# Lower halves of 34 expert tiles split beside the mixers and kept in DRAM, with 34 early first products in layer 0 and 16 of their results in DRAM

## The chip, the cores and the metric

The kernel runs on one core of one Trainium2 chip. The metric is the device time in microseconds of one execution. The kernel before takes 3050.3 us (median of 3 runs, 3050.26 to 3050.61).

## What the reference computes

The reference is a two-layer backbone (`DEPTH = 2`) over 256 latent and 256 context tokens of width 1024. Each layer modulates and normalises the tokens, projects them, runs four token mixers side by side, gates and sums their outputs, and then runs PEER, a retrieval over 16384 single-neuron experts in a 128 x 128 grid of product keys. Layer 0 treats all 512 tokens in PEER, layer 1 the 256 latent ones. The part that matters here:

```
s = einsum('thpd,hpnd->thpn', q, keys);  sv, si = top_k(s, 16)       # 8 heads, two lists of 128 keys
best, pos = top_k(sums of the two lists, 16);  g = softmax(best)     # 16 experts of each head
act = gelu(einsum('tkd,td->tk', u_tab[ec], xc))                      # first product, with U
out = einsum('tk,tkd->td', gc * act, v_tab[ec])                      # second product, with V
```

The kernel does not gather the rows of most tokens. It treats the experts as 128 tiles of 128. For each tile it forms the first product of all its tokens with all 128 experts, multiplies the gelu of it by a gate that is zero where an expert was not chosen, and adds the second product. In layer 0, 384 of the 512 tokens go this way; the first 128 tokens go by gathering their rows, on GpSimd and VectorE (`gather`).

## The kernel before

**Numbers.** Every fp32 matrix is split into an upper half `wh` (rounded to fp32r by a ScalarE copy) and a lower half `wl` (the rest, by a VectorE subtraction). A product is three fp32r matmuls: upper by upper, upper by lower, lower by upper (`mm3`, L391 to L393). So every 512 KB weight tile that arrives in the buffer `wraw` costs one ScalarE and one VectorE instruction of 128 x 1024 before TensorE can use it. `wraw`, `wh` and `wl` have three buffers each.

**Stages of a layer.** First the mixers with their projections, then an output projection (`out`), queries (`wq`), routing, and the expert loop. Instructions are issued engine by engine in an order that a scheduler fixes when the program is built; each engine and each DMA queue then runs its own row in that order.

- *Mixers (layer 0: up to about 570 us).* A list made by `unit_order` names the weight tiles in the order of use: `na`, `gqa`, `dif`, then 32 `gate` tiles with `hyn` among them, and from gate 0 on one `modr` tile (a row block of the modulation matrix, consumed by VectorE at L513) behind each gate. `Units.load` (L305) brings them into `wraw` on the SP queue; `Units.split` (L328, L329) makes the halves, for some tiles on GpSimd, which takes longer.
- *Routing (layer 0: about 643 to 873 us).* Per group of 128 tokens VectorE ranks keys (`lists`, `top16`), picks experts (`select`), and builds one-hot matrices (`hot`, L1501, `gated`, L1517) from which TensorE scatters the gates (`scatter`, L1539), which ScalarE evacuates into `gblk` and SP stores to `gd`. Beside it `early` runs first products as a filler: one call of `u_next` per step of the routing. `u_next` loads a tile of U (L1227), splits it (L1230, L1231), multiplies 24 matmuls of 384 columns and takes the gelu (L1257) into one of `ne` result buffers. `NE = (20, 50)` limits the early products of layer 0 to 20: 10 buffers of their own and 10 in `hT`, which is free at that time.
- *Expert loop (layer 0: from about 873 us).* For j in 0..127: load V and the gates, multiply gelu by gate (L1666), split the result and V, 18 matmuls of 512 columns for the second product (L1677), and `u_next` for a tile further on, when a result buffer is free and the tile is at most `own + ...` ahead. Behind the split of V a few steps of `gather` are taken: two per j, and every second j a third from j = 25 on. A step of `gather` issues a row gather on GpSimd's queue and adds or dots an earlier one on VectorE (L1307, L1311); three buffers `grow`.

Of the kernel before, what the change touches and what calls it, by code (L numbers as in the profile page):

```python
# [8 lines left out]
F32 = mybir.dt.float32  # L9
# [10 lines left out]
P = 128  # L20
# [44 lines left out]

def unit_order():

    o = []
    for l in range(DEPTH):
        o += [(l, 'na', i) for i in range(6)]  # L70
        o += [(l, 'gqa', i) for i in range(4)]
        o += [(l, 'dif', i) for i in range(6)]
# [69 lines left out]
def lay_out(i):  # L142
# [59 lines left out]
    a['W'] = np.stack([U[k] for k in dict.fromkeys(order)])  # L202
# [57 lines left out]
NE_BUF = (10, 18)  # L260
NE_OWN = (10, 34)
NE = (20, 50)
# [4 lines left out]
def body(ctx, tc, I, out, dbg=None):  # L267
# [26 lines left out]
    place = {k: z for z, k in enumerate(dict.fromkeys(order))}  # L294

    class Units:
# [4 lines left out]
        def load(self, upto):  # L301
            while self.loaded < min(upto, len(order)):
                m = self.loaded
                self.raw[m] = wp.tile([P, D], F32, name="wraw", bufs=3)
                sp.dma_start(self.raw[m], I['W'][place[order[m]]])  # L305
# [12 lines left out]
        def split(self, upto):  # L318
            while self.split_to < min(upto, len(order)):
# [9 lines left out]
                (pool if order[m][1] == 'wq' or order[m][:2] == (1, 'na') and order[m][2] < 2 or order[m][0] == 0 and order[m][1] in ('gate', 'hyn') and order[m][2] % 2 and (order[m][1] == 'hyn' or order[m][2] < 20) else dve).tensor_tensor(lo, r, h.bitcast(F32), op=ALU.subtract)  # L329
                self.hl[m] = (h, lo)  # L330
# [7 lines left out]
        def next(self, kind):  # L338
            assert order[self.n][1] == kind, (order[self.n], kind)

            end = kind == 'wq' and order[self.n + 1:self.n + 2] != [(order[self.n][0], kind, (order[self.n][2] + 1) % 8)]
            self.split(self.n + (1 if end else 2))
# [229 lines left out]
    for l in range(DEPTH):  # L572
# [647 lines left out]
        assert own == nbuf or last  # L1220
        gd = [dr.tile([NB, P, 32, 32], F32, name=f"gd{l}_{z}") for z in range(4)]
        us, ur, gas = {}, {}, {}
# [10 lines left out]
        def split_u(j):  # L1233
# [3 lines left out]
            lo = wp.tile([P, D], F32R, name="wl", bufs=3)  # L1237
            halves(h, lo, ur.pop(j), lo_eng[0])
            us[j] = (h, lo)

        def u_mm(j):
# [97 lines left out]
        with ExitStack() as tx:  # L1339
# [238 lines left out]
            def routing():  # L1578
# [46 lines left out]
        with ExitStack() as dx:  # L1625
# [29 lines left out]

            def gate(j):
# [3 lines left out]
                if z < own:  # L1660
# [45 lines left out]
            mrows = mod_rows()  # L1706
            load_v(0)
# [4 lines left out]
            for j in range(P):  # L1712
                load_v(j + 2)
                load_g(j + 4)

# [115 lines left out]
```

## Time and profile before

| What | Value |
|---|---|
| median of 3 runs | 3050.3 us |
| the profiled execution | 3045.44 us, its span 3043.6 us |
| TensorE (PE) busy | 2934.7 us, 96% |
| VectorE (DVE) busy | 2270.8 us, 75% |
| ScalarE (ACT) busy | 1457.9 us, 48% |
| GpSimd (POOL) busy | 515.4 us, 17% |
| DMA | 661.95 MB, mean 217 GB/s |
| granted TensorE clock, mean | 0.988 |

The share of busy time is a mean over stages with different limits. Matmuls overlap in the pipeline, so the time that one costs TensorE is the distance from its start to the start of the next, which is shorter than its duration; a stretch in which PE is shown busy all the time can therefore still have room.

### The profile page before, as it was taken

Reading aid. Unit: us, or ns where it says so; the run is one execution under the profiler, and the core shown is the slowest. Engines: PE = TensorE matmul, PEld = TensorE weight load, DVE = VectorE, ACT = ScalarE, POOL = GpSimd, SP = SyncE. Lnnn points to the kernel's source line nnn. Section 1 sums busy time; section 2 is a strip of 40 time slices with the busy share of each in tenths; the row PEclk is TensorE's granted clock in tenths of the full one; section 3 lists DMA queues with packets and bytes.
Section 4 is the critical chain, followed back from the end, with each engine's and each line's share of the span. In section 5 each row is a group of like instructions: output and inputs, shape, how many; then the busy total and the mean of one; then the engine's idle time right before and its main releaser. Section 6 shows DMA issues by size and latency. Waiting matters only on the chain.

```text
span 3043.6 us, 47372 instructions
## 1 busy us (share of the span) xinstructions
PE 2934.7 (96%) x17500; PEld 2595.1 (85%) x17500; DVE 2270.8 (75%) x4818; ACT 1457.9 (48%) x2583; POOL 515.4 (17%) x374
## 2 busy tenths in 40 slices
PE   8999999988899999999999998999899999999998
PEld 6877777888799999999999986888898989989986
DVE  5775877799988777778777686789699667555545
ACT  5444422558853333333333334465548754555443
POOL 1001100220023444434444101000160000000000
PEclk9999999999999999999999998999999999999999
DMA  7232345534489998898998864357655699766644
GB/s 273 74 103 85 111 140 163 177 99 173 160 309 341 332 322 302 309 333 313 316 321 311 280 190 140 91 181 223 198 164 199 214 298 307 227 208 208 210 149 146
DMA packets 263032, 661.95 MB, mean 217 GB/s; under 512 B 21480, under 2 KB 114160, under 8 KB 262288
## 3 DMA queue, kind: packets, MB, share of 16 engines
q1 hardware_dynamic: 222336, 513.88, 51.4%
q0 software_dynamic: 40464, 145.05, 13.8%
q8 instruction: 137, 2.24, 0.3%
q14 instruction: 95, 0.78, 0.1%
HBM read 609.56 MB, written 49.29 MB: 216 GB/s over the span
## 4 chain that ended last, share of the span: by engine, by line
PE 68%; DVE 11%; DMA 4%; issue 2%; ACT 2%; POOL 0%; DVEq 0%; ACTq 0%; SPq 0%; POOLq 0%
PE mm L1677 13%; PE at L1677 13%; PE po L393 9%; PE po L391 9%; PE po L392 9%; PE mm L391 4%; PE mm L392 4%; PE mm L393 4%; PE at L1539 3%; DMA vr<-in_V_dram 2%; DMA wraw<-in_W_dram 2%; DVE wl L1231 1%; DVE wl L329 1%; ACT vh L1230 1%; DVE rep L1364 1%
## 5 line engine op out<-in xcount | busy, mean ns | idle before, releaser
L393 PE MATMUL po<-nh,wl 128*128 128x384 f32 (+1 forms) x2048 | 635.7, 311 | 10.6 <-DVE wl L1231 10.5
L391 PE MATMUL po<-nh,wh 128*128 128x384 f32 (+1 forms) x2048 | 638.0, 312 | 7.3 <-ACT wh L1230 3.5
L1230 ACT ACTIVATE wh<-wraw 128x1024 fp32r<-128x1024 f32 x256 | 270.5, 1058 | 338.8 <-PE po L392 283.7
L1230 ACT ACTIVATE vh<-vr 128x1024 fp32r<-128x1024 f32 x254 | 269.7, 1062 | 304.5 <-DMA vr<-in_V_dram 265.6
L391 PEld LDWEIGHTS po<-nh,wh 128*128 128x128 f32 x2048 | 390.5, 191 | 17.0 <-ACT wh L1230 4.5
L393 PEld LDWEIGHTS po<-nh,wl 128*128 128x128 f32 x2048 | 390.1, 191 | 13.8 <-DVE wl L1231 13.1
L1231 DVE TENSOR_TENSOR vl<-vr,vh 128x1024 fp32r<-128x1024 f32 x254 | 310.2, 1221 | 110.3 <-ACT vh L1230 110.1
L1231 DVE TENSOR_TENSOR wl<-wraw,wh 128x1024 fp32r<-128x1024 f32 x241 | 293.6, 1220 | 114.3 <-ACT wh L1230 113.9
L391 PE MATMUL mm<-nh,wh 128*128 128x256 f32 (+1 forms) x1056 | 346.7, 330 | 12.2 <-ACT nh L488 3.9
L392 PE MATMUL po<-nl,wh 128*128 128x384 f32 x1024 | 344.6, 337 | 0.0
L393 PE MATMUL mm<-nh,wl 128*128 128x256 f32 (+1 forms) x1056 | 341.8, 325 | 0.4 <-POOL wl L329 0.4
L392 PE MATMUL mm<-nl,wh 128*128 128x256 f32 (+1 forms) x992 | 324.3, 328 | 0.2 <-DVE nl L472 0.2
L328 ACT ACTIVATE wh<-wraw 128x1024 fp32r<-128x1024 f32 x156 | 164.7, 1058 | 291.1 <-PE mm L392 166.4
L392 PE MATMUL po<-nh,wh 128*128 128x256 f32 x1024 | 289.8, 283 | 0.0
L1300 POOL DMA_INDIRECT grow<-in_UR_dram,gix x128 | 173.8, 1358 | 481.2 <-DVE gix L1473 240.4
L1677 PE MATMUL mm<-vl,Wh 128*128 128x512 f32 x635 | 250.2, 394 | 4.3 <-DVE vl L1231 4.2
L1677 PE MATMUL mm<-vh,Wh 128*128 128x512 f32 x635 | 248.3, 391 | 1.6 <-ACT vh L1230 1.6
L1677 PE MATMUL at<-vh,Wl 128*128 128x512 f32 x635 | 248.5, 391 | 0.0
L1677 PE MATMUL at<-vh,Wh 128*128 128x512 f32 x635 | 248.2, 391 | 0.0
L1677 PE MATMUL mm<-vh,Wl 128*128 128x512 f32 x635 | 247.5, 390 | 0.0
L1677 PE MATMUL at<-vl,Wh 128*128 128x512 f32 x635 | 247.1, 389 | 0.0
L391 PEld LDWEIGHTS mm<-nh,wh 128*128 128x128 f32 x1056 | 203.5, 193 | 38.5 <-ACT nh L471 4.7
(367 smaller groups left out, 6200.7 us busy)
## 6 DMA issues: line engine op xcount, KB each, us to landing
wraw<-in_U_dram SPq DMA_DIRECT2D x256, 512.0 KB, 4.5
vr<-in_V_dram SPq DMA_DIRECT2D x254, 512.0 KB, 4.6
wraw<-in_W_dram SPq DMA_DIRECT2D x214, 512.0 KB, 3.8
gd<-gblk SPq DMA_DIRECT2D x80, 512.0 KB, 4.5
G<-gd SPq DMA_DIRECT2D x32, 768.0 KB, 8.1
G<-gd SPq DMA_DIRECT2D x32, 512.0 KB, 5.4
grow<-in_W_dram SPq DMA_DIRECT2D x24, 512.0 KB, 4.5
mw<-in_W_dram SPq DMA_DIRECT2D x16, 512.0 KB, 9.3
```

The costliest lines, as they stand in the source:

```text
L328: act.activation(h, r, AF.Copy)
L329: (pool if order[m][1] == 'wq' or order[m][:2] == (1, 'na') and order[m][2] < 2 or order[m][0] == 0 and order[m][1] in ('gate', 'hyn') and ...
L391: pe.matmul(ps, w[0], x[0], start=first, stop=False)
L392: pe.matmul(ps, w[0], x[1], start=False, stop=False)
L393: pe.matmul(ps, w[1], x[0], start=False, stop=last)
L1230: act.activation(h, r, AF.Copy)
L1231: return eng.tensor_tensor(lo, r, h.bitcast(F32), op=ALU.subtract)
L1300: pool.indirect_dma_start(out=q[-1], out_offset=None, in_=tab, in_offset=bass.IndirectOffsetOnAxis(ap=gix[:, p, e:e + 1], axis=0))
L1364: dve.match_replace(rep[:, :nn], v[:, 0:8], x, -3e38)
L1539: pe.matmul(ps4[:, :, z], A[:, :, z], C[:, z, :, h], start=h == 1, stop=h == 0)
L1677: pe.matmul(accs[i][h], w[a][:, i * 128:(i + 1) * 128], v[b][:, h * 512:(h + 1) * 512], start=j == 0 and a + b == 0, stop=j == P - 1 and a ...
```

## The change

- `unit_order` puts 34 units `('pre', j)` between the projection tiles of layer 0: one before each of `na` 1 to 5, `gqa` 0 to 3, `dif` 0 to 5, `hyn` 0 to 5, and `gate` 12 to 24. A `pre` unit loads tile j of U, splits it like any other (ScalarE copy, VectorE subtraction), and stores the lower half to DRAM (`ulo_d`). Its upper half is dropped.
- In routing, `load_u` brings, for j below 34, the tile of U on SP's queue and the stored lower half on GpSimd's queue into `wl`; `split_u` then makes only the upper half, on ScalarE.
- The early first products of layer 0 go from 20 to 34: `NE` is now 18 (8 own buffers and 10 in `hT`), and the gelu of the first 16 goes through a tile `gs` (two buffers) to DRAM (`ga_d`). The expert loop loads them back, two iterations ahead (`load_ga`).
- The steps of `gather` are spread anew: one per j for j from 2 to 19, then 2 or 3 (two of three j's take 3).

```diff
+N_PRE = (34, 0)
         for i in range(32):
             if i == 8:
-                o += [(l, 'hyn', i) for i in range(6)]
-            o += [(l, 'gate', i)]
+                o += proj('hyn', 6)
+            o += [(l, 'pre', j) for j in [next(pre, None) if 11 < i < 28 else None] if j is not None] + [(l, 'gate', i)]
...
-NE_BUF = (10, 18)
-NE_OWN = (10, 34)
-NE = (20, 50)
+NE_BUF = (8, 18)
+NE_OWN = (8, 34)
+NE = (18, 50)
+
+NE_OUT = (16, 0)
...
+                if order[m][1] == 'pre':
+                    sp.dma_start(ulo_d[order[m][0]][order[m][2]], lo.bitcast(F32))
+                    continue
...
         def load_u(j):
                 sp.dma_start(ur[j], I['U'][l, j])
+                if j < N_PRE[l]:
+                    ul[j] = wp.tile([P, D], F32R, name="wl", bufs=3)
+                    pool.dma_start(ul[j], ulo_d[l][j])
...
+            if j < N_PRE[l]:
+                lo = ul.pop(j)
+                act.activation(h, ur.pop(j), AF.Copy)
+            else:
...
+            if j < nout:
+                ga = up.tile([P, nd], F32, name="gs", bufs=2)
+                tables.append(act.activation(ga, ps[:, :nd], AF.Gelu))
+                sp.dma_start(ga_d[j], ga)
+                return
...
-                    fill.add(early(own + 2048 // nd))
+                    fill.add(early(nout + own + 2048 // nd))
...
-                        fill.add(early(ne - 2 if NG else ne))
+                        fill.add(early(nout + ne - 2 if NG else ne))
-                fill.add(early(ne))
+                fill.add(early(nout + ne))
...
+            def load_ga(j):
+                if j < nout:
+                    gas[j] = None, up.tile([P, nd], F32, name="gs", bufs=2)
+                    sp.dma_start(gas[j][1], ga_d[j])
...
-                        for _ in range((2 if j > 1 else 0) + (j > 24 and j % 2)):
+                        for _ in range((j > 1) if j < 20 else 2 + (j % 3 > 0)):
```

Three places in the order of the built programs follow. The line numbers of the changed kernel are some 30 higher.

ScalarE in the last scatter of layer 0, in the kernel before (`gblk` is the evacuation of scattered gates, `wh` the upper half of a U tile, `hT<-po` the gelu of a first product into `hT`):

```order
L1541 ACTIVATE gblk<-at 128x128x4 x2
L1515 ACTIVATE ohC<-ohB,gT 128x128
L1545 ACTIVATE gacc<-gblk 128x64
L1515 ACTIVATE ohC<-ohB,gT 128x128 x3
L1541 ACTIVATE gblk<-at 128x128x4 x8
L1545 ACTIVATE gacc<-gblk 128x64
L1230 ACTIVATE wh<-wraw 128x1024
L1257 ACTIVATE hT<-po_8994 128x384
```

The same place in the changed kernel:

```order
L1571 ACTIVATE gblk<-at 128x128x4 x2
L1260 ACTIVATE wh<-wraw 128x1024
L1287 ACTIVATE hT<-po_9354 128x384
L1571 ACTIVATE gblk<-at 128x128x4 x2
L1260 ACTIVATE wh<-wraw 128x1024
L1287 ACTIVATE hT<-po_9414 128x384
L1545 ACTIVATE ohC<-ohB,gT 128x128 x4
```

Where eight evacuations stood in a row with no product between them, every two are now followed by a product. On TensorE the first second product stands behind 527 matmuls of first products (22 tiles) before, and behind 816 (34 tiles) now.

SP's queue beside the gates 12 to 24, before (`wraw<-in_W` brings a gate or modulation tile, `wbraw` a branch tile):

```order
L305 DMA wraw<-in_W_dram 128x1024 x2
L308 DMA wbraw<-in_WB_dram 128x256
L305 DMA wraw<-in_W_dram 128x1024 x3
L308 DMA wbraw<-in_WB_dram 128x256
L305 DMA wraw<-in_W_dram 128x1024 x2
```

And now (`ulo` is the stored lower half of a U tile):

```order
L341 DMA ulo_26_95<-wl 128x1024
L315 DMA wraw<-in_U_dram 128x1024
L315 DMA wraw<-in_W_dram 128x1024 x2
L318 DMA wbraw<-in_WB_dram 128x256
L341 DMA ulo_27_96<-wl 128x1024
L315 DMA wraw<-in_U_dram 128x1024
```

Each gate now has three tiles through the three `wraw` buffers where it had two, and a store that waits for a VectorE subtraction stands ahead of the loads.

VectorE a few iterations into the expert loop, before (`vl` is the lower half of V, `Wl` that of the gated gelu, `grow,gdot` a gathered row):

```order
L1307 SCALAR_TENSOR_TENSOR grow,gdot<-grow,mtok 128x1024 x2
L1231 TENSOR_TENSOR wl<-wraw,wh 128x1024
L1666 TENSOR_TENSOR ga<-ga,G_9149 128x384
L1231 TENSOR_TENSOR vl<-vr,vh 128x1024
L1231 TENSOR_TENSOR Wl<-ga,Wh 128x384
```

And now:

```order
L1337 SCALAR_TENSOR_TENSOR grow,gdot<-grow,mtok 128x1024
L1703 TENSOR_TENSOR gs<-gs,G_9921 128x384
L1252 TENSOR_TENSOR vl<-vr,vh 128x1024
L1252 TENSOR_TENSOR Wl<-gs,Wh 128x384
```

For its first 21 iterations the loop now holds second products alone on TensorE (378 matmuls in a row), one gathered row in each, and no split of U.

## Rows read from the trace of the kernel before

**Rows 1.** The page: busy us, share of the span and instructions of the engines.
```profile
PE 2934.7 (96%) x17500; PEld 2595.1 (85%) x17500; DVE 2270.8 (75%) x4818; ACT 1457.9 (48%) x2583; POOL 515.4 (17%) x374
```

**Rows 2.** Busy time by stretch of layer 0 (columns: first row).
```profile
core 0: us, PE busy (x) PEld busy (x) DVE busy (x) ACT busy (x) POOL busy (x), PEclk, DMA share, GB/s
36.00:170.00 134.00, 130.24 (x852) 105.69 (x850) 96.44 (x313) 69.55 (x151) 11.60 (x19) 1.00 0.36 106
336.00:450.00 114.00, 109.80 (x503) 87.06 (x502) 92.75 (x194) 38.69 (x66) 11.73 (x5) 0.97 0.41 129
643.00:668.00 25.00, 17.83 (x104) 16.59 (x103) 25.00 (x122) 10.54 (x16) 0.00 (x0) 0.88 0.20 64
668.00:723.00 55.00, 45.35 (x334) 41.52 (x334) 51.10 (x179) 50.12 (x141) 0.00 (x0) 0.96 0.40 144
723.00:780.00 57.00, 53.66 (x365) 49.90 (x362) 51.63 (x192) 45.96 (x120) 0.00 (x0) 0.97 0.46 167
780.00:805.00 25.00, 21.95 (x149) 19.87 (x148) 21.02 (x87) 19.39 (x48) 0.00 (x0) 0.93 0.41 148
805.00:873.00 68.00, 61.79 (x426) 58.88 (x423) 65.36 (x211) 48.25 (x108) 0.00 (x0) 0.95 0.57 217
873.00:1798.00 925.00, 924.94 (x4677) 840.53 (x4676) 712.97 (x917) 333.29 (x455) 346.38 (x256) 1.00 0.89 311
1798.00:1823.00 25.00, 25.00 (x113) 20.79 (x112) 23.93 (x46) 10.08 (x15) 0.00 (x0) 1.00 0.60 188
```

**Rows 3.** Timeline of TensorE in the expert loop: second product, first product, second product.
```profile
1500.50 0.39 PE L1677 MATMUL mm<-vh,Wh 128*128 128x512 f32 x1
...
1504.59 0.34 PE L391 MATMUL po<-nh,wh 128*128 128x384 f32 x1
...
1508.75 0.39 PE L1677 MATMUL mm<-vh,Wh 128*128 128x512 f32 x1
```

**Rows 4.** Timeline of TensorE: first first product, first second product of layer 0.
```profile
642.85 0.34 PE L391 MATMUL po<-nh,wh 128*128 128x384 f32 x1
...
873.35 0.50 PE L1677 MATMUL mm<-grow,Wh 128*128 128x512 f32 x1
```

**Rows 5.** Groups of instructions, 640 to 870 us: busy us, mean ns, idle before.
```profile
L1539 PEld LDWEIGHTS <-ohA 128*128 128x128 f16 x768 | 85.6, 139 | 26.2 <-issue 18.1 <-DVE ohA L1501 6.3 <-DVE ohC L1517 0.5
L1231 DVE TENSOR_TENSOR wl<-wraw,wh 128x1024 fp32r<-128x1024 f32 x22 | 26.6, 1212 | 1.1 <-ACT wh L1230 1.1
```

**Rows 6.** The splits of weights beside the mixers, 36 to 450 us.
```profile
L329 DVE TENSOR_TENSOR wl<-wraw,wh 128x1024 fp32r<-128x1024 f32 x32 | 39.0, 1220 | 20.8 <-ACT wh L328 20.7
L328 ACT ACTIVATE wh<-wraw 128x1024 fp32r<-128x1024 f32 x45 | 47.6, 1058 | 99.0 <-issue 45.6 <-PE mm L392 40.5 <-PE mm L393 8.2
```

**Rows 7.** Upper halves and VectorE's longest wait, 336 to 450 us.
```profile
L328 ACT ACTIVATE wh<-wraw x12: 1051/1060/1064, 336.2 to 443.6; 128x1024 fp32r<-128x1024 f32 x12
DVE junk L513 <- DMA wraw<-in_W_dram: 10.2, 5, 3.5
```

**Rows 8.** DMA of 336 to 450, of 880 to 950, of 1800 to 1824 us.
```profile
wraw<-in_W_dram SPq DMA_DIRECT2D x25, 512.0 KB, 3.8
...
DMA packets 13465, 24.08 MB, mean 344 GB/s; under 512 B 697, under 2 KB 8583, under 8 KB 13461
vr<-in_V_dram SPq DMA_DIRECT2D x10, 512.0 KB, 6.9
grow<-in_UR_dram,gix POOLq DMA_INDIRECT x21, 7.3
...
vr<-in_V_dram SPq DMA_DIRECT2D x3, 512.0 KB, 4.0
```

**Rows 9.** VectorE in the expert loop, 870 to 1800 us.
```profile
L1307 DVE SCALAR_TENSOR_TENSOR grow<-grow,mtok 128x1024 f32<-128x1024 f32 x128 | 154.4, 1221 | 82.8 <-DMA grow<-in_UR_dram,gix 82.8
L1231 DVE TENSOR_TENSOR Wl<-ga,Wh 128x384 fp32r<-128x384 f32 x102 | 56.3, 552 | 13.0 <-ACT Wh L1230 12.8
```

**Rows 10.** DMA on GpSimd's queue beside the mixers, 36 to 170 us.
```profile
qk<-in_cst_dram POOLq DMA_DIRECT2D x1, 512.0 KB, 11.3
```

More of the change, by code (lines that the diff above doesn't have):

```diff
@@ L69, in unit_order @@
     for l in range(DEPTH):
-        o += [(l, 'na', i) for i in range(6)]
-        o += [(l, 'gqa', i) for i in range(4)]
-        o += [(l, 'dif', i) for i in range(6)]
+        pre = iter(range(N_PRE[l]))
+        proj = lambda kind, n: [x for i in range(n) for x in [(l, 'pre', j) for j in ([] if kind == 'na' and i == 0 else
+                                                                                       [next(pre, None)]) if j is not None] + [(l, kind, i)]]
+        o += proj('na', 6)
+        o += proj('gqa', 4)
+        o += proj('dif', 6)
         for i in range(32):
             if i == 8:
-                o += [(l, 'hyn', i) for i in range(6)]
-            o += [(l, 'gate', i)]
+                o += proj('hyn', 6)
+            o += [(l, 'pre', j) for j in [next(pre, None) if 11 < i < 28 else None] if j is not None] + [(l, 'gate', i)]
             if N_MOD1 + i < (N_MOD2 if l else N_MOD):
@@ L201, in lay_out @@
     order = unit_order()
-    a['W'] = np.stack([U[k] for k in dict.fromkeys(order)])
+    a['W'] = np.stack([U[k] for k in dict.fromkeys(order) if k[1] != 'pre'])
     a['WB'] = np.stack(WB)
@@ L293, in body @@
     order = unit_order()
-    place = {k: z for z, k in enumerate(dict.fromkeys(order))}
+    place = {k: z for z, k in enumerate(k for k in dict.fromkeys(order) if k[1] != 'pre')}
+    ulo_d = [[dr.tile([P, D], F32, name=f"ulo{l}_{j}") for j in range(N_PRE[l])] for l in range(DEPTH)]
     class Units:
@@ L304, in load @@
                 self.raw[m] = wp.tile([P, D], F32, name="wraw", bufs=3)
-                sp.dma_start(self.raw[m], I['W'][place[order[m]]])
+                sp.dma_start(self.raw[m], I['U'][order[m][0], order[m][2]] if order[m][1] == 'pre' else I['W'][place[order[m]]])
                 if order[m][1] == 'gate':
@@ L338, in next @@
         def next(self, kind):
+            if order[self.n][1] == 'pre':
+                self.split(self.n + 2)
+                self.n += 1
             assert order[self.n][1] == kind, (order[self.n], kind)
             end = kind == 'wq' and order[self.n + 1:self.n + 2] != [(order[self.n][0], kind, (order[self.n][2] + 1) % 8)]
-            self.split(self.n + (1 if end else 2))
+            self.split(self.n + (1 if end else 2 + (order[min(self.n + 1, len(order) - 1)][1] == 'pre')))
             if not end:
@@ L1220, in body @@
         assert own == nbuf or last
+        nout = NE_OUT[l]
         gd = [dr.tile([NB, P, 32, 32], F32, name=f"gd{l}_{z}") for z in range(4)]
-        us, ur, gas = {}, {}, {}
+        us, ur, ul, gas = {}, {}, {}, {}
+        ga_d = [dr.tile([P, nd], F32, name=f"ga{l}_{z}") for z in range(nout)]
         def load_u(j):
@@ L1236, in split_u @@
             h = wp.tile([P, D], F32R, name="wh", bufs=3)
-            lo = wp.tile([P, D], F32R, name="wl", bufs=3)
-            halves(h, lo, ur.pop(j), lo_eng[0])
+            if j < N_PRE[l]:
+                lo = ul.pop(j)
+                act.activation(h, ur.pop(j), AF.Copy)
+            else:
+                lo = wp.tile([P, D], F32R, name="wl", bufs=3)
+                halves(h, lo, ur.pop(j), lo_eng[0])
             us[j] = (h, lo)
@@ L1659, in gate @@
                 z, ga = gas.pop(j)
-                if z < own:
+                if z is None:
+                    pass
+                elif z < own:
                     free.insert(0, z)
@@ L1706, in body @@
             mrows = mod_rows()
+            load_ga(0)
+            load_ga(1)
             load_v(0)
@@ L1714, in body @@
                 load_g(j + 4)
+                load_ga(j + 2)
                 while nu[0] < min(P, j + own + (ne - own) * max(0, 64 - j) // 64) and free:
```

## Prediction

> **What bounds the kernel now.** The page comes first: TensorE is busy 96% of the span [rows 1], so only a stage in which it has room can pay for anything. The busy time by stretch, read second, finds that room [rows 2]. In the expert loop PE is shown busy 924.94 of 925 us. In routing (643 to 873 us) it is VectorE that is full: 25.00 of 25, 51.10 of 55, 51.63 of 57, 21.02 of 25, 65.36 of 68 us, 214.1 of 230 together.
>
> How much room TensorE really has there takes the pitch of its matmuls, from the timeline, third. A second product of one tile runs from 1500.50 to 1504.59, a first product from there to 1508.75: 4.09 and 4.16 us [rows 3]. The 768 scatter matmuls keep the weight loader busy 85.6 us [rows 5]. Routing lasts from the first first product at 642.85 to the first second product at 873.35, 230.5 us [rows 4]; in it stand 22 first products (91.5 us), the scatter (85.6) and some 5 us of small matmuls: 182 us. So 48 us of TensorE lie open in routing, on a stage that VectorE sets. 26.6 us of VectorE's time there are 22 subtractions of U's lower half [rows 5].
>
> **The change part by part.**
>
> *First products moved into routing.* 34 tiles instead of 22 are done before the first second product, 12 more, so the expert loop after it holds 12 x 4.16 = 49.9 us less of TensorE. As TensorE has no gap in that loop [rows 2], this comes off in full: -49.9.
>
> *Routing grows by less than that.* I go by stretches. Up to 805 us the four stretches take 162 us with 148.8 us of VectorE, 92% [rows 2]. 16 of the 22 subtractions lie there (about 18.3 us of the 26.6); without them VectorE has 130.5 us, at the same 92% 142 us. TensorE's own work there is 15 first products (62) and 512 scatter matmuls (57) and a little more, 122 us, and fits. The last scatter now has 19 first products beside 256 scatter matmuls: 19 x 4.16 + 256 x 85.6/768 = 79.0 + 28.5 = 107.5 us, and 2 for its ends, where TensorE sets the pace instead of VectorE (the ranking of the last group of tokens moves up into it). Sum 142 + 110 = 252 us against 230.5: +22. From below, TensorE's work alone is 34 x 4.16 + 85.6 + 5 = 232 us, +2; VectorE at its old share with nothing saved by overlap gives 260, +30. I take +22, since the middle stretches stay VectorE's.
>
> *The stores and loads of 16 gelus* (192 KB each) lie beside TensorE's 4 to 6 us per product in routing; the covers are two `gs` buffers and DMA shares of 0.41 to 0.57 there [rows 2]. Zero; if that cover is gone it is the case of the late halves below.
>
> *The loop's first 21 iterations* are second products alone, 4.09 us each. VectorE needs 1.22 (lower half of V) + 2 x 0.55 + 1.3 (a gathered row) = 3.6 us of that [rows 6, 9], still below. The loads are nearer: V 512 KB, the returned gelu 192, a quarter of the gates' 768, a gathered row 512, together 1.44 MB in 4.09 us, 353 GB/s; from 880 to 950 us the DMA engines moved 344 GB/s on the mean [rows 8]. And V has two buffers: landing (6.9 us under that load, 4.0 in the quiet tail [rows 8]), the copy 1.06, the subtraction 1.22 and the issue make 6.6 to 9.5 us for two iterations, 3.3 to 4.8 each. Bounds: 0, and 21 x 0.7 = 15. At the end of the loop TensorE runs second products alone with no gap, 113 matmuls in 25.00 us [rows 2], but at 188 GB/s. I take 0.3 an iteration, +6, between the two landings.
>
> The Trainium skill ("DMA: Bandwidth & Descriptors", section "Where 436 GB/s comes from") puts the HBM's limit for one core near 358 GB/s, which binds between HBM and SBUF. By that figure 353 GB/s would just pass and this term would be 0 from bandwidth; by the row's 344 GB/s bandwidth alone costs 2 us. The trace's mean agrees with the figure as a ceiling.
>
> *The rest of the loop.* Rows are gathered at 2.67 per iteration instead of 2.5; VectorE already waits 0.65 us for each (82.8 over 128) [rows 9]. Its work per iteration of 8.25 us rises by 0.17 x 1.3 = 0.2 us. Hidden as long as the split of V runs one iteration ahead, as now. Zero, at most 95 x 0.14 = 13.
>
> *34 tiles of U beside the mixers.* Each costs 1.22 us of VectorE and 1.06 of ScalarE [rows 6], a 512 KB load and store on SP. VectorE has cover of 38 us in 36 to 170 us (15 tiles, 18 us) [rows 2]; the six at `hyn` lie in 240 to 290 us, after which the gates follow. The dear place is gates 12 to 24. There VectorE is busy 92.75 of 114 us [rows 2] and a gate comes every (443.6 - 336.2)/11 = 9.8 us [rows 7]; 13 tiles add 15.9 us, so VectorE goes from 81% to 95%. Two buffer rings get tighter as well. Behind a gate's load stood one other tile in the three `wraw`; now all three are taken in each period, so the load of a gate waits for the split of the one before it: landing 3.8 [rows 8], copy 1.06, subtraction 1.22, issue 0.4, about 6.5 us plus VectorE's lag, against 9.8. And ScalarE's copy of the next `pre` tile waits for TensorE to leave the gate before (now it waits like that for one two gates back). Queued behind on SP is the store that waits for a subtraction, with the loads of the next three tiles after it; TensorE waits for those. VectorE loses 10.2 us here to such landings already, in five waits [rows 7]. I take 0.6 us for each of the 13 gates, 8, and 4 for the start, where weights and 5 tiles of U share the queue: +12. Below: 0, all covered. Above: all VectorE time on the path, 34 x 1.22 = 41.5, and 4: 45.
>
> Sum: -49.9 + 22 + 6 + 0 + 12 = -9.9 us. The profiled execution took 3045.44 us (span 3043.6 and 1.8 around it), so it would take 3035.5; the median of the runs stands 4.9 above it at 3050.3, so the forecast is **3040.4 us**.
>
> **The rivals.**
>
> *The mixers cover all* (chance 0.22). VectorE's shares of 72% and 81% speak for it, the waits on landings in [rows 7] against it. With 0 there, 1 in the loop and routing at +20: -29, 3021 us.
>
> *Gates 12 to 24 become bound by VectorE and the `wraw` ring* (0.17). One mechanism: VectorE, filled to 95%, lags; every lag delays the split, that the next load, that the next split. It decides when the lag passes 9.8 - 6.5 = 3.3 us, or when VectorE's lost landings double. Price at the upper bound, 45: -49.9 + 22 + 6 + 45 = +23, 3073 us, slower than before. The saturated stretch speaks for it; that TensorE already idles little there speaks against.
>
> *The loop starves* (0.10). V alone goes at 4.8 us per iteration and the denser gathers lag: 15 + 13 beside 12 and 22: +12, 3062 us. For it: 344 GB/s with landings of 6.9 us. Against it: no gap of TensorE in that load today.
>
> *The lower halves come late, so that the early products are not early* (0.06). They come on GpSimd's queue; `wl` has three buffers, so the load of tile j+2 starts when product j-1 ends, and between back-to-back products (4.16 us each, some 9 in a row in the middle of routing) it has 8.3 us. A 512 KB load on that queue took 11.3 us once [rows 10], row gathers 7.3 [rows 8]. At 11.3 nine products wait 3 us each: +27, 3067 us. The skill gives such a rule ("SBUF — State Buffer", in "The DVE blocks DMA trap (SWDGE)"): descriptors of GpSimd's queue aren't written while VectorE holds the port pair they share. No row here shows it.
>
> *Savings and costs cancel* within 6 us, with none of these: 0.05.
>
> **How the numbers follow.** The forecast has 0.40; its own range is 3028 to 3053. A change below 0.2% (6 us) can't be told from none. Faster by more: 0.22 + 0.40 x 0.75 + 0.02 = 0.54. Within: 0.40 x 0.2 + 0.05 + a share of the starved loop and late halves, 0.19. Slower: the rest, 0.27. The range of 8 in 10 leaves out the upper half of the saturated gates and the lower part of full cover: 3017 to 3067 us.
>
> **What would show it.** Routing, from the first first product to the first second product, takes 252 us, with VectorE near 75% in it. The first 21 second products come every 4.4 us. `na` to `wq` end 12 us later, and the gap is at gates 12 to 24, in VectorE's waits for `wraw`. The forecast is wrong if the first first product starts over 25 us later than 642.85, or if routing takes over 265 us.

## The result and the profile after

The changed kernel takes 3079.61 us (median of 5 runs, 3070.81 to 3087.26), the kernel before 3050.26 (5 runs, 3045.99 to 3050.61). The ratio is 1.0098, 95% interval 1.0080 to 1.0117: slower by 29 us, where 3040.4 was forecast and the range ended at 3067. The profiled execution has a span of 3077.8 us against 3043.6, so 34.2 us more.

First the page: the engines, and the chain that ended last (by engine, then by line).

```profile
PE 2954.4 (96%) x17500; PEld 2605.3 (85%) x17500; DVE 2279.5 (74%) x4818; ACT 1487.0 (48%) x2617; POOL 536.8 (17%) x408
...
PE 59%; DVE 11%; issue 11%; DMA 5%; POOL 5%; ACT 3%; SPq 0%; POOLq 0%; DVEq 0%; ACTq 0%
PE mm L1714 9%; PE at L1714 9%; PE po L409 7%; PE po L407 7%; PE po L408 7%; POOL grow L1330 4%; PE mm L407 4%; PE mm L408 4%; PE mm L409 4%; PE at L1569 3%; DMA wraw<-in_W_dram 2%; DMA vr<-in_V_dram 2%; PE at L403 1%; DVE wl L339 1%; DVE rep L1394 1%
```

TensorE's share is the 96% of [rows 1]. What is to be seen is one entry of the chain: `POOL grow L1330`, GpSimd's issue of row gathers, with 4% of the span, and "issue" with 11%. GpSimd is busy 17% of the time, as before, and nothing in a list of busy shares would point to it. In the chain of the kernel before, POOL has 0% and "issue" 2%:

```profile
PE 68%; DVE 11%; DMA 4%; issue 2%; ACT 2%; POOL 0%; DVEq 0%; ACTq 0%; SPq 0%; POOLq 0%
```

Next the turning points, on TensorE's timeline (start us, us, what, idle before): the first product of the `dif` scores, the first first product, the first second product, and one stall inside the loop.

```profile
175.25 0.48 PE L723 MATMUL at<-qk 64*128 64x256 f32 x1
...
666.62 0.34 PE L407 MATMUL po<-nh,wh 128*128 128x384 f32 x1
...
922.37 0.39 PE L1714 MATMUL mm<-grow,Wh 128*128 128x512 f32 x1
...
1288.21 0.39 PE L1714 MATMUL at<-vh,Wl 128*128 128x512 f32 x1
1293.54 0.69 PE L407 MATMUL po<-nh,wh 128*128 128x384 f32 x1 [4.94 <-ACT ga L1287]
1294.02 0.53 PE L408 MATMUL po<-nl,wh 128*128 128x384 f32 x1
...
1297.49 0.34 PE L407 MATMUL po<-nh,wh 128*128 128x384 f32 x1
```

Against [rows 4] the first first product comes 23.8 us later (666.62 for 642.85), the first second product 49.0 later: the mixers lost 23.8, routing 25.3 (255.75 for 230.50). From the first to the last second product layer 0 takes 949.4 us against 967.3, so the loop gives back 17.9. Between the layers 3.2 are added, and layer 1 is as before: 23.8 + 25.3 - 17.9 + 3.2 = 34.4.

The last rows show what a stall costs: TensorE stood 4.94 us, then ran its matmuls in 0.53 us instead of 0.34 until 1297.49. The granted clock of those 4 us is 0.51 (a row of the next fence), the lower of the two levels, 1.2 GHz. That iteration took 15.22 us instead of 8.25, 7.0 for a gap of 5.

Busy time by stretch (columns as in [rows 2]):

```profile
36.00:170.00 134.00, 122.50 (x754) 99.51 (x752) 99.53 (x297) 77.02 (x145) 11.56 (x19) 0.95 0.62 205
667.00:922.00 255.00, 240.26 (x1654) 227.08 (x1654) 198.50 (x775) 192.50 (x455) 17.97 (x33) 1.00 0.72 256
922.00:1010.00 88.00, 82.16 (x350) 65.26 (x349) 67.56 (x105) 31.86 (x42) 19.06 (x19) 0.98 0.99 348
1100.00:1350.00 250.00, 236.44 (x1161) 211.26 (x1159) 188.22 (x277) 77.00 (x109) 112.24 (x82) 0.98 0.91 317
1293.50:1297.50 4.00, 3.96 (x13) 3.96 (x14) 3.38 (x7) 3.21 (x6) 2.23 (x2) 0.51 0.87 305
1400.00:1700.00 300.00, 300.00 (x1528) 274.11 (x1527) 236.90 (x243) 102.30 (x144) 138.94 (x97) 1.00 0.91 318
```

The first row is the mixers' start: PE 122.50 of 134 us for 130.24 in [rows 2], clock 0.95, DMA share 0.62 for 0.36. In routing (second row) TensorE and VectorE changed places: 240.26 and 198.50 of 255 us, and the clock is full. In the loop 1100 to 1350 us has lost its full TensorE, and 1400 to 1700 us, with the same gathers per iteration and the same GB/s, has not.

To place the loss I take each iteration of the loop and subtract 4.08 us for its second product and 4.17 for a first product if it has one. Without stalls the loop is 964.3 us before and 914.2 after, 50.1 less. Left over:

| stalls in layer 0's loop, us | iterations 0 to 19 | 20 to 69 | 70 to the end | all |
|---|---|---|---|---|
| before | 0.5 | 0 | 2.5 | 3.0 |
| after | 9.4 | 25.0 | 0.9 | 35.3 |

The groups of the gathers in 1100 to 1350 us (busy us, mean ns, idle before and its releasers), first on VectorE, then on GpSimd:

```profile
L1337 DVE SCALAR_TENSOR_TENSOR grow<-grow,mtok 128x1024 f32<-128x1024 f32 x82 | 99.5, 1224 | 61.8 <-DMA grow<-in_UR_dram,gix 61.3
...
L1330 POOL DMA_INDIRECT grow<-in_UR_dram,gix x80 | 109.6, 1370 | 135.9 <-DVE grow L1337 129.9 <-issue 6.1
L1330 POOL DMA_INDIRECT grow<-in_V_dram,gix x2 | 2.6, 1309 | 3.4 <-DVE grow L1337 3.4
```

They wait for each other: VectorE for the gathered row, GpSimd for VectorE to free a row buffer. 82 issues in 250 us are 3.05 us a gather. VectorE's 188.22 us of work and its 61.8 of waiting fill the stretch, so the halves of V and U behind a late row come late. The waits of TensorE in the same stretch (us, times, longest):

```profile
PE po L407 <- ACT ga L1287: 6.5, 2, 4.9
PE mm L1714 <- DVE vl L1252: 4.1, 2, 2.8
PE po L409 <- DVE wl L1252: 2.1, 1, 2.1
```

The top line would send a reader to ScalarE's gelu, or to a shortage of result buffers. ScalarE's timeline at the stall shows that the gelu itself stood behind the copy of a V tile whose load came late:

```profile
1291.11 1.06 ACT L1251 ACTIVATE vh<-vr 128x1024 fp32r<-128x1024 f32 x1 [15.01 <-DMA vr<-in_V_dram]
1292.07 1.04 ACT L1251 ACTIVATE wh<-wraw 128x1024 fp32r<-128x1024 f32 x1
1293.02 0.47 ACT L1287 ACTIVATE ga<-po 128x384 f32<-128x384 f32 x1
```

That load was issued at 1276.49 us, right behind a load of 2 MB (`hT`) in SyncE's queue:

```profile
1272.89 3.50 SPq L1765 DMA_DIRECT2D hT<-h  x1
1276.49 0.38 SPq L1668 DMA_DIRECT2D vr<-in_V_dram  x1
```

The stall of iteration 61, 6.7 us, has another last link. The gelu of the gathered products stands in ScalarE's row ahead of the next split of U, and waits there until VectorE has used the last of the 128 gathered rows of U:

```profile
1351.10 0.31 ACT L1344 ACTIVATE gdot<-gdot 128x128 f32<-128x128 f32 x1 [9.02 <-DVE grow L1337]
```

These two stalls hold 13.6 of the 25.0 us. The kernel before has both waits too: there the V load behind `hT` took 13.9 us to land, and that gelu waited 8.75 us, and TensorE lost nothing by either. So a lead that covered them is gone. Whether the late rows took it can't be read from the list of waits; the experiments tell.

### The profile page after: what moved, and what is told of

Read it like the earlier page. It is cut to its first block, busy times and chain, and to the rows that moved or that the text cites. A ratio compares the mean times of both kernels' runs of the same rounds, so it can differ in the third digit from the quotient of the medians.

```text
span 3077.8 us, 47737 instructions
## 1 busy us (share of the span) xinstructions
PE 2954.4 (96%) x17500; PEld 2605.3 (85%) x17500; DVE 2279.5 (74%) x4818; ACT 1487.0 (48%) x2617; POOL 536.8 (17%) x408
## 4 chain that ended last, share of the span: by engine, by line
PE 59%; DVE 11%; issue 11%; DMA 5%; POOL 5%; ACT 3%; SPq 0%; POOLq 0%; DVEq 0%; ACTq 0%
PE mm L1714 9%; PE at L1714 9%; PE po L409 7%; PE po L407 7%; PE po L408 7%; POOL grow L1330 4%; PE mm L407 4%; PE mm L408 4%; PE mm L409 4%; PE at L1569 3%; DMA wraw<-in_W_dram 2%; DMA vr<-in_V_dram 2%; PE at L403 1%; DVE wl L339 1%; DVE rep L1394 1%
## 5 line engine op out<-in xcount | busy, mean ns | idle before, releaser
L1252 DVE TENSOR_TENSOR wl<-wraw,wh 128x1024 fp32r<-128x1024 f32 x207 | 252.5, 1221 | 114.2 <-ACT wh L1251 114.0
L339 DVE TENSOR_TENSOR wl<-wraw,wh 128x1024 fp32r<-128x1024 f32 x151 | 184.0, 1220 | 62.5 <-ACT wh L338 51.3
```

The lines of the kernel that those rows point to most:

```text
L1252: return eng.tensor_tensor(lo, r, h.bitcast(F32), op=ALU.subtract)
```

## The experiments

"Loop" is from the first to the last second product of layer 0, "start" the first first product, both from the profiled execution. Ratios are to the kernel before, on the same chip, with 95% intervals. Medians are of 4 to 12 runs (e16: 2) on several chips, on which the kernel before took 3046.3 to 3051.0 us, so rows are compared by their ratios.

| kernel | median us | ratio | start | loop | stalls 0 to 19 | 20 to 69 | 70 on |
|---|---|---|---|---|---|---|---|
| before | 3050.3 | 1 | 642.8 | 967.3 | 0.5 | 0 | 2.5 |
| changed | 3079.6 | 1.0098 (1.0080 to 1.0117) | 666.6 | 949.4 | 9.4 | 25.0 | 0.9 |
| e1 gathers by pace | 3063.0 | 1.0063 (1.0045 to 1.0080) | 669.9 | 927.4 | 8.9 | 0 | 4.3 |
| e2 old gather rule | 3080.8 | 1.0111 (1.0094 to 1.0128) | 668.2 | 951.9 | 25.1 | 11.7 | 0.9 |
| e3 before, new gather rule | 3068.2 | 1.0076 (1.0060 to 1.0093) | 644.2 | 984.6 | 0.5 | 17.6 | 2.3 |
| e4 nothing beside na, gqa | 3058.1 | 1.0038 (1.0018 to 1.0058) | 651.2 | 949.5 | 9.3 | 22.4 | 3.7 |
| e5 4 row buffers | 3056.8 | 1.0033 (1.0023 to 1.0042) | 665.9 | 927.2 | 8.8 | 3.1 | 0.9 |
| e6 3 V buffers | 3098.4 | 1.0164 (1.0149 to 1.0178) | 669.6 | 983.3 | 8.2 | 39.2 | 21.9 |
| e7 e1 and e4 | 3043.5 | 0.9988 (0.9979 to 0.9997) | 645.5 | 930.8 | 12.3 | 0 | 4.3 |
| e8 e7, middle to DRAM | 3059.5 | 1.0036 (1.0024 to 1.0048) | 646.8 | 953.3 | 12.9 | 10.8 | 15.6 |
| e9 e4, e5, pace of 3 | 3046.6 | 0.9991 (0.9980 to 1.0001) | 648.2 | 933.9 | 10.5 | 0 | 9.3 |
| e10 e5, no gathers to 19 | 3061.5 | 1.0037 (1.0025 to 1.0048) | 670.0 | 931.9 | 4.2 | 0 | 13.4 |
| e11 stores by GpSimd | 3113.8 | 1.0206 (1.0187 to 1.0226) | 700.6 | 951.0 | 11.3 | 24.6 | 1.0 |
| e12 no lower halves | 3079.5 | 1.0093 (1.0075 to 1.0112) | 642.2 | 958.5 | 10.6 | 26.9 | 6.9 |
| e13 9 not stored | 3093.7 | 1.0160 (1.0138 to 1.0183) | 673.2 | 943.6 | 8.0 | 20.4 | 0.9 |
| e14 9 only loaded | 3096.0 | 1.0151 (1.0132 to 1.0169) | 663.4 | 962.4 | 14.8 | 29.0 | 4.4 |
| e15 e4, e5, pace of 2.67 | 3045.0 | 0.9986 (0.9975 to 0.9997) | 649.1 | 926.6 | 8.4 | 2.6 | 1.5 |
| e16 9 loaded by 1/16 | 3086.4 | 1.0116 (1.0072 to 1.0159) | 664.8 | 950.5 | 14.9 | 15.6 | 5.9 |

**The rate of the gathers (e1, e2, e3).**

```
 e1   n0 = nu[0]            # before the loop's first products of this iteration
      pace = (2.67 if nu[0] > n0 else 1) * (j > 1);  credit[0] += pace
-     for _ in range((j > 1) if j < 20 else 2 + (j % 3 > 0)):
+     for _ in range(int(credit[0]) - int(credit[0] - pace)):
 e2 +     for _ in range((2 if j > 1 else 0) + (j > 24 and j % 2)):
 e3 the kernel before with
    +     for _ in range((j > 1) if j < 20 else 2 + (j % 3 > 0)):
```

> The changed kernel, but an iteration of layer 0's expert loop that has no first product asks for 1 row gather instead of 2 or 3. Theory R (gathers are asked for faster than their three row buffers pass them): in the changed kernel's iterations 20 to 63, 117 gathers are asked for in 334 us of matmuls, 2.85 us each, while GpSimd issued one per 3.05 us there (82 in 1100 to 1350 us); 117 x 3.05 - 334 = 23 us of stalls, 26 measured. With 106 gathers, 3.15 us each, under 6 us of them should be left: 3057 us (3052 to 3062). Rival S (result buffers: 8 instead of 10 of the loop's own, and the waits for a gelu in front of first products): gathers play no part, 3079 us, stalls where they were.

> The changed kernel with the old rule of gathers (2 per iteration from the second on, 2 or 3 from the 25th). Theory R: iterations 2 to 23 ask for 46 gathers in 106 us of matmuls and need 46 x 3.05 = 140 us, so some 34 us of stalls come in the first 25 iterations, and those of iterations 30 to 63 go (97 gathers in 297 us, 3.05 us each): 3080 to 3090 us. Rival S: stalls stay at iterations 30 to 63, and the time stays at 3079 us.

> The kernel before with the new rule of gathers alone (1 per iteration to the 19th, then 2 or 3, mean 2.67). Theory R: iterations 20 to 63 ask for 117 gathers in 334 us as in the changed kernel, so up to 23 us of stalls come into a loop that had none: 3065 to 3073 us. Rival S: the kernel before has its 10 result buffers, no stalls, 3050 us.

e1 takes the 25 us of stalls in iterations 20 to 69 away and leaves none there. The stretch of about iterations 20 to 63, 1013 to 1368 us, in e1:

```profile
1013.00:1368.00 355.00, 355.00 (x1787) 321.70 (x1787) 272.78 (x400) 129.81 (x176) 158.94 (x113) 1.00 0.91 320
```

PE is busy 355.00 of 355 us; the changed kernel has 338.63 in the same stretch, at nearly as many gathers (113 and 116). The median of 3063.0 is 6 above the 3057 expected; 3 of them lie in the mixers, which ended later in its profile than in the changed kernel's. By the ratios e1 gains 0.35%, 11 us, where its profiled loop is 22 shorter; single profiles don't resolve that difference. e3 does the reverse: the new rule alone, in the kernel before with its ten result buffers, makes 17.6 us of stalls in the same iterations. e2 moves stalls to the front as theory R has it, though 25 us rather than 34 there, and 12 that were not expected stay behind. Rival S, the result buffers, is out by e1 and e3: they were not touched in either. The chain of the page agrees: POOL has 5% in e3 as in the changed kernel, and 1% in e1.

**Ring or bandwidth (e5, e6).**

```
 both  NE_BUF 8 -> 5, NE_OWN 8 -> 5, NE 18 -> 15, NE_OUT 16 -> 19   (layer 0)
 e5    name="grow", bufs=3  ->  bufs=4 - l
 e6    name="vr", bufs=2 -> bufs=3;  load_v(j + 2) -> load_v(j + 3)
```

> The changed kernel with 4 row buffers for the gathers instead of 3; the room comes from 3 result buffers (5 instead of 8), and 19 results instead of 16 go to DRAM, so 34 first products stay early. Theory R1 (the ring of row buffers: issue 1.4 us, flight about 7 us, VectorE 1.3 us, 9.2 us over 3 buffers = 3.05 us a gather): 4 buffers pass one per 2.3 to 2.5 us, and the 25 us of stalls in iterations 20 to 63 go: 3050 to 3058 us. Rival R2 (the bandwidth of the DMA engines, 0.91 busy there, sets 3.05 us): another buffer only waits longer, the stalls stay within 5 us, 3075 to 3083 us. Rival S (result buffers): with 5 of them more stalls, over 3085 us.

> The changed kernel with 3 buffers for V tiles instead of 2 and the load three iterations ahead, room and DRAM results as in the kernel with 4 row buffers. It is about the 9 us lost in the first 20 iterations, where second products stand alone at 4.08 us. Theory V1 (ring of V buffers: flight about 7 us, ScalarE 1.06, VectorE 1.22, 9.2 us over 2 buffers = 4.6 us an iteration): 3 buffers give 3.1 us and the 9 us go to under 2. Rival V2 (bandwidth: 1.44 MB asked for per 4.08 us, 353 GB/s, at a DMA share of 0.97 to 1.0): they stay at 7 to 10. Iterations 20 to 63 keep 20 to 30 us of stalls by either.

One more row buffer, with fewer result buffers, empties iterations 30 to 69 of stalls without a change of rule. e6 shares its result buffers and keeps 39.2 us of stalls there, so it is the row buffer that does it. GpSimd's gathers and the busy times of e5 in the window shown above:

```profile
L1330 POOL DMA_INDIRECT grow<-in_UR_dram,gix x74 | 109.1, 1475 | 94.2 <-DVE grow L1337 85.0 <-issue 7.6 <-DVE Wl L1252 1.5
L1330 POOL DMA_INDIRECT grow<-in_V_dram,gix x17 | 23.9, 1405 | 25.5 <-DVE gacc L1341 15.2 <-DVE grow L1337 7.9 <-issue 2.4
```

```profile
1100.00:1350.00 250.00, 250.00 (x1261) 226.81 (x1261) 207.29 (x292) 89.70 (x122) 131.90 (x91) 1.00 0.97 354
```

91 gathers instead of 82, one per 2.75 us, at 354 GB/s instead of 317 and with TensorE full. So 317 GB/s at a share of 0.91 was no ceiling: the ring of three buffers was, and R2 falls. The Trainium skill ("DMA: Bandwidth & Descriptors", "Where 436 GB/s comes from") puts one core's HBM limit near 358 GB/s. This row's mean stays under it, but shorter stretches don't: the changed kernel moved 367 GB/s from 922 to 955 us (a row below) and the kernel before 401 from 880 to 897.5. Here, where one core runs, the measurement decides: the figure is no ceiling.

e6 went the wrong way. In the first 20 iterations 8.2 us stay, the number of V2, so a third V buffer isn't what they lacked; but 61 us of stalls come later, on to iteration 110. That one load further ahead of V holds up the rows or U's tiles behind it is a guess; no run separates it.

**The first 20 iterations (e8, e10).**

```
 e8  -     if j < nout:             (in u_mm and load_ga)
     +     if own <= j < own + nout:          ga_d[j] -> ga_d[j - own]
     the limit of first products:  j + own + (nout + ne - own) * max(0, 64 - j) // 64
 e10 (on e5)  pace = (3 if nu[0] > n0 else 1) * (j >= 20)
```

> As the kernel with both mendings, but products 8 to 23 go to DRAM instead of 0 to 15, so that the loop's own 8 buffers come free from iteration 0 and 8 of the first 24 iterations have a first product: fewer second products alone in a row. If the 9 us of the first 20 iterations come from DMA demand of second products alone, they fall to under 5, and the ratio is 0.997 to 0.999 of the kernel before; if from the reload of results from DRAM, they stay and the ratio is as with the two mendings.

> As the kernel with 4 row buffers, but no gathers at all in the first 20 iterations, then 3 (1 in an iteration without a first product). Read are the first 20 iterations only, since the gathers then end late and cost something at the loop's end. Theory T (traffic: V, gates, results from DRAM and a gather are 1.44 MB per 4.08 us, 353 GB/s): without gathers it is 225 GB/s, and of the 9 us lost in iterations 0 to 19 under 2 are left. Rival U (the reload of results from DRAM with two buffers, behind other loads on SyncE's queue): 7 to 9 us stay.

e10 fits neither expectation: 4.2 us are left of e5's 8.8, in this stretch (926 to 1008 us):

```profile
926.00:1008.00 82.00, 79.41 (x345) 63.98 (x344) 50.49 (x72) 30.38 (x41) 2.67 (x2) 1.00 0.87 278
```

The gathers are half of the loss; with them the changed kernel's stretch runs at 348 GB/s and a share of 0.99 (922 to 1010 us above). The other half comes at 278 GB/s, where VectorE waits 9.3 us in all for gates from DRAM and 1.7 for results between 972 and 1004 us. Bandwidth alone doesn't explain either half. The changed kernel's first eight iterations moved 367 GB/s, more than the 353 that theory T counts, with TensorE full; its loss comes behind them, at 336:

```profile
922.00:955.00 33.00, 33.00 (x148) 27.25 (x147) 23.65 (x34) 13.52 (x17) 7.53 (x7) 1.00 1.02 367
955.00:1010.00 55.00, 49.16 (x204) 38.01 (x203) 43.91 (x72) 18.34 (x25) 11.53 (x12) 0.97 0.97 336
```

e8 failed: first products spread over the first 24 iterations brought more stalls, not fewer. Its limit lets the lead fall over 64 iterations, so it has short iterations and full gathers mixed further on; that part stays open.

**The mixers (e4, e11, e12, e13, e14, e16).**

```
 e4  no 'pre' beside 'na' and 'gqa';  beside gates 3 to 10 and 12 to 25
 e11 -     sp.dma_start(ulo_d[...], lo)      +  pool.dma_start(ulo_d[...], lo)
 e12 N_PRE = (0, 0)
 e13 tiles 0 to 8: split, not stored;  halves again in routing
 e14 tiles 0 to 8: loaded, not split;  e16: of each only columns 0 to 63 loaded
```

> The changed kernel, but the 9 lower halves made beside the na and gqa units are made beside gates instead (gates 3 to 10 and 12 to 27; none beside na and gqa). Theory P (the place costs: na and gqa stand where the DMA share rose from 0.48 to 0.75, and lost 16 of the 24 us): the first first product comes at 650 to 658 us instead of 666.6, and the time is 3063 to 3071 us. Rival Q (each tile costs the same wherever it is made): 666 us and 3079 us.

> The changed kernel, but the lower halves made beside the mixers are stored from GpSimd's queue instead of SyncE's. Theory Q (the store waits in SyncE's queue for its lower half, and the next weight loads stand behind it: 81 us of such waits at the store in 36 to 190 us): the first first product comes at 650 to 658 us instead of 666.6, the time is 3063 to 3071 us. Rival W (the work and traffic of the extra tiles themselves, or the store's place in GpSimd's queue): 664 to 670 us, 3077 to 3083 us.

> The changed kernel without any lower halves beside the mixers: all 34 are made by VectorE in the routing. First first product at 643 us (666.6 before this edit). Theory D (VectorE bounds the routing again, 34 x 1.22 = 41 us of work on top of the 198 of 255 us that it is busy): routing 265 to 275 us, loop 949, in all 3064 to 3074 us. Rival E (TensorE bounds it, 240 of 255 us busy, and VectorE's 57 us of room take them): routing 256 to 260 us, 3054 to 3059 us.

> The changed kernel, but the 9 lower halves made beside na and gqa are not stored; VectorE makes them again in the routing. Theory Q (the store in SyncE's queue holds the next loads up): the first first product comes at 650 to 656 us (666.6 with the store, 645 to 651 without these tiles). Rival L (the extra load and the weight buffer that it takes, 3 for all): 664 to 669 us. Rival H (the extra work of ScalarE and VectorE, 2.28 us a tile): 664 to 669 us as well. The routing takes up to 9 x 1.22 = 11 us more than 256.

> As the kernel without these stores, but the 9 tiles are only loaded beside na and gqa, and not split: no ScalarE or VectorE work, no store, no buffers for halves. Rival L: 662 to 669 us for the first first product. Rival H: it falls to 645 to 651 us. Theory Q: 645 to 652, as little as with the halves.

> As the kernel whose 9 tiles beside na and gqa are only loaded, but each load brings 64 of 1024 columns: 32 KB instead of 512 KB into the same buffer. Read is the start of the first dif product, 161.2 us in the kernel before and 172 us with the full loads. Theory B (the buffer: with 3 weight buffers every second one goes to a tile that no mixer uses, so a unit's load starts one unit later): it stays at 168 to 174 us. Rival T (traffic, DMA share 0.75 against 0.48 before): 161 to 165 us.

(The range of e4's edit goes to gate 27, as its expectation says; the 34 tiles end at gate 25.) Three marks place the delay: a side product of the `hyn` filter that runs behind the five tiles beside `na`, the first `dif` score behind all nine, and the start.

| us | behind `na` | first `dif` score | start |
|---|---|---|---|
| before | 80.66 | 161.23 | 642.8 |
| without the nine: e4, e7 | 82.60, 80.17 | 166.69, 164.14 | 651.2, 645.5 |
| e16, 1/16 loaded | 88.61 | 169.67 | 664.8 |
| e14, loaded | 91.99 | 172.19 | 663.4 |
| e13, split, not stored | 95.01 | 178.65 | 673.2 |
| changed | 92.52 | 175.25 | 666.6 |

The rows of the first mark in the changed kernel, e14 and e16:

```profile
92.52 0.48 PE L681 MATMUL at<-k,qk 128*128 128x256 f32 x1 [1.23 <-DVE k L673]
```

```profile
91.99 0.44 PE L683 MATMUL at<-k,qk 128*128 128x256 f32 x1
```

```profile
88.61 0.48 PE L686 MATMUL at<-k,qk 128*128 128x256 f32 x1
```

Against the mean of e4 and e7 the nine tiles cost 11.1, 9.8 and 18.3 us at the three marks. Loaded only, they still cost 10.6, 6.8 and 15.0; with 1/16 of the bytes, 7.2, 4.3 and 16.4. So at the two marks right behind these tiles, four to seven tenths of it hang on what e16 leaves of a tile: a buffer out of three, an issue on SyncE's queue and 32 KB. No run gave the mixers a fourth buffer, so that it is the buffer is argued and not shown. e13 shows no gain from leaving the store out, against theory Q; its start of 673.2 lies above all three expectations. From the `dif` score to the start the price grows by 8 to 12 us in the changed kernel, e14 and e16 alike, behind tiles that all three treat the same. No run tells why, so the start can't weigh the parts of these nine tiles.

What is firm is the place. Six profiles with the changed kernel's order (it, e1, e2, e5, e6, e10) start at 665.9 to 670.0 us, five with e4's order (e4, e7, e8, e9, e15) at 645.5 to 651.2. Within one order they differ by 4 to 6 us, so how traffic and halves share the remainder isn't settled. In 36 to 100 us e16 has nearly the DMA share of before and still the lower clock:

```profile
36.00:100.00 64.00, 59.08 (x336) 46.97 (x335) 34.89 (x69) 32.65 (x53) 4.17 (x7) 0.95 0.49 145
```

(before: share 0.47, clock 1.00, PE 62.24.) The queue of SyncE in e16 shows every other load to be U's, with a buffer that a weight would have had:

```profile
63.49 0.33 SPq L316 DMA_DIRECT2D wraw<-in_U_dram  x1
63.93 0.37 SPq L318 DMA_DIRECT2D wraw<-in_W_dram  x1
66.67 0.33 SPq L316 DMA_DIRECT2D wraw<-in_U_dram  x1
67.10 1.33 SPq L321 DMA_DIRECT2D wbraw<-in_WB_dram  x3
68.48 0.42 SPq L318 DMA_DIRECT2D wraw<-in_W_dram  x1
71.94 0.33 SPq L316 DMA_DIRECT2D wraw<-in_U_dram  x1
```

e11 was worse by 34 us. GpSimd's queue also holds lower halves of `hyn` and gates, and a store that waits for VectorE stands in front of them (36 to 480 us):

```profile
POOL ulo L341 <- DVE wl L339: 169.5, 19, 20.4
POOL wl L339 <- ACT wh L338: 84.1, 10, 19.6
```

This shows only that GpSimd's queue is no better place; of SyncE's it says nothing. Neither start that was expected came (650 to 658, 664 to 670; it is 700.6), and the rival W fits by its second clause alone.

e12 weighs the lower halves as a whole: without them the mixers are those of before (642.2), and routing takes 271.6 us instead of 255.75, inside the 265 to 275 of theory D. 24.4 us won and 15.8 lost; the 9 us that the loop added are stalls in other places, so the total came out above the expected 3064 to 3074, equal to the changed kernel's. In e13 the first 9 halves alone cost routing 10.7 us, 1.19 each: they probably stand where VectorE still sets the pace. The difference to e12 leaves 5.1 for the other 25.

**The versions put together (e7, e9, e15).** All have e4's order; e7 adds e1's pace, e9 and e15 add e5's buffers with a pace of 3 and 0.5, or 2.67 and 1.

> Both mendings at once: gathers by pace (1 in an iteration without a first product, else 2.67) and no lower halves beside na and gqa. If the two losses are independent they add up: against the kernel before, 1.0098 - 0.0035 - 0.0060 = 1.0003, so +1 us (-3 to +5). If they feed one another (lower halves late, loop later) the ratio comes out above 1.003.

> 4 row buffers (5 result buffers, 19 results in DRAM), gathers by pace (3 in an iteration with a first product, 1 in two iterations without), no lower halves beside na and gqa. If the ring of row buffers set the stalls of iterations 20 to 63 and transfers asked for by second products alone those of the first 20, the loop has 914 us of matmuls and under 6 us of stalls, against 931 us for the loop with pace and three row buffers: 3029 to 3036 us, ratio 0.993 to 0.996. If it was not the traffic that cost the first 20 iterations, their 9 to 12 us stay and the ratio is 0.998 to 0.999.

> 4 row buffers, no lower halves beside na and gqa, gathers by pace with 2.67 instead of 3 in an iteration with a first product and 1 in one without. A gather per 3.09 us instead of 2.75 leaves the 8 us of stalls in iterations 80 to 109 out; the 9 to 11 us of the first 20 stay: loop 925 to 930 us, 3035 to 3044 us, ratio 0.996 to 0.999. If those 8 us come from the reload of hT at iteration 80 and not from the gathers, the ratio is 0.999 as with 3.

The two losses add up: e7 comes to 0.9988, a little under the 1.0003 of the added ratios. e9 misses the under 6 us of stalls that it was to show if traffic set the first 20 iterations: 10.5 us stay there, and 9 come after iteration 70 with its 3 gathers per iteration. With 2.67 (e15) those 9 are gone, and the loop of 926.6 us is the shortest. e7 and e15 beat the kernel before by 0.12 and 0.14%, with intervals that end at 0.9997. Of the 50 us saved, routing takes 25, the mixers 3 to 6, the first 20 iterations 8 to 12, the rest of the loop 4 and the stretch between the layers 2 to 9.

## Why the prediction was wrong

By its terms, forecast and measured in the profiled executions:

| term | forecast | measured | shown by |
|---|---|---|---|
| first products out of the loop | -49.9 | -50.1 | 94 first products in it for 106, at 4.17 us |
| routing | +22 | +25.3 | timeline |
| second products alone at the start | +6 | +8.9 | iterations 0 to 19 |
| the rest of the loop, denser gathers | 0 (bound 13) | +23.4 | e1, e3, e5 |
| lower halves beside the mixers | +12 (0 to 45) | +23.8 | e4, e12, e14, e16 |
| between the layers, layer 1 | 0 | +3 | not tested |
| sum | -9.9 | +34 | |

*What held.* The saving was there in full (counted: 12 first products fewer in the loop). Routing took 255.75 us for 252, with VectorE at 78% (198.50 of 255) where "near 75%" was foreseen, and TensorE sets its pace. The early losses of second products alone came where they were put, half again as large. Late lower halves, the rival on GpSimd's queue, did not happen: TensorE's weight loads wait 1.1 us in all for them in 667 to 922 us, with VectorE busy 78% of it, so the trap that the forecast cited from the Trainium skill ("SBUF — State Buffer", "The DVE blocks DMA trap (SWDGE)") had no visible price here:

```profile
L409 PEld LDWEIGHTS po<-nh,wl 128*128 128x128 f32 x271 | 51.3, 189 | 1.1 <-DMA wl<-ulo 1.1
```

Neither sign of being wrong that the forecast named came: the first first product started 23.8 us later, not over 25, and routing took 255.75 us, not over 265. It had none for the loop behind its first 21 iterations, where over half of the miss lies (23.4 of 44 us by the table).

*What failed first.* "The rest of the loop ... Zero, at most 95 x 0.14 = 13." That step weighed 0.17 gathers more per iteration of 8.25 us in VectorE's time, and found 0.2 us. Two things were left out. An iteration without a first product lasts 4.08 us and asks for just as many gathers, and 7 of the 44 iterations from 20 to 63 are such: 117 gathers in 334 us, 2.85 us each. And a gather isn't priced by VectorE's 1.3 us but by the ring it runs in. In 1100 to 1350 us of the kernel before it takes 7.0 us from issue to landing (GpSimd's 1.3 of issue are in it), 0.9 until VectorE takes the row, 1.2 there and 0.5 until GpSimd issues into the freed buffer: 9.6 us over three buffers, 3.2 us each. The changed kernel passed one per 3.05. 117 x 3.05 - 334 = 23 us, and 25 are measured; the 3.05 come from a stretch with such stalls in it, so the proof is e1, e3 and e5 and not this sum. The rows for it were there: the old rule asked for 97 gathers in 297 us, 3.06 each, so it was already at the ring's limit, and the 82.8 us that VectorE waited [rows 9] were read as room where they were the sign of it. GpSimd's row in the kernel before shows the other side, 1100 to 1350 us: it too waits for VectorE to free a row.

```profile
L1300 POOL DMA_INDIRECT grow<-in_UR_dram,gix x61 | 81.4, 1334 | 113.0 <-DVE grow L1307 107.9 <-issue 4.3 <-DVE hT L1666 0.8
```

"The loop starves" named lagging gathers, with V as the cause and 28 us in the loop for both. 32 were measured, 23 of them from the gathers, and no run shows the two V buffers as the cause of the other 9 (e6).

*What failed second.* The mixers' +12 was put 4 at the start and 8 at gates 12 to 24. 14 of the 23.8 us were lost before `dif`. The forecast saw the ring of three `wraw` at the gates ("now all three are taken in each period") and covered the start with VectorE's 38 us of room. But e14, which takes VectorE's work for the nine early tiles away, still starts 15 us later than e4 and e7: room on VectorE was no cover for what a tile takes from the loads. e4's order, with 22 tiles beside gates where the change has 13, loses 3 to 8 us in all, so the gates were not the dear place, and the mark "the gap is at gates 12 to 24" was wrong too.

*A reading to set right.* The forecast took the mean of 344 GB/s [rows 8] as agreeing with a ceiling of 358. Within that same stretch the kernel before moved 401 GB/s from 880 to 897.5 us, so the mean hid that transfers can run faster. The 6 us for the early iterations stand on the two V buffers and not on this ceiling. They came near the 8.9 measured by luck: a third V buffer (e6) left the loss there.

*Left open.* What sets the loss in iterations 0 to 19 beside the gathers, what undid e6 and e8, why the price of the nine early tiles grows behind the `dif` score, and the 3 us between the layers, which the other kernels also show (604.6 to 614.7 us from the last second product of layer 0 to the first of layer 1, 606.0 before). Executions of the changed kernel spread over 16 us, those of e3, which has only the new rule, over 7.

## What to carry to other kernels

Price a background stream in the ring it runs in: issue, flight and use together, over the number of its buffers, set against the time between requests in the shortest iterations, not the usual ones. A prefetch with no work of its own still takes a buffer in every ring that it passes through, so look there before counting the engines' room. And where a wait names an engine, take the suspected buffers up or down by one: one more row buffer (e5) settled what the list of waits put on ScalarE's gelu.

## What the runs showed of the hardware

The DMA engines carried 354 GB/s over 250 us at a share of 0.97 with no stall of TensorE (e5), and 367 over 33 us (922 to 955 us of the changed kernel), where 317 at 0.91 with stalls had looked like a limit. A V load of 512 KB took 13.9 us to land behind a load of 2 MB in the same queue (kernel before, issued at 1295.35 us), where the median of its kind was 6.4 in 1100 to 1350 us. A gap of 4.94 us on TensorE was followed by 4 us at a granted clock of 0.51, the lower level, so that stall cost 7.0 us. Taking 15/16 of the bytes out of nine loads (e16 against e14) gave back 3.4 us at the mark behind `na` and nothing at the start, 664.8 for 663.4: a load can cost much of its price without its bytes.
